# A two-block transformer forward pass on one NeuronCore: its state-space model computed in blocks of eight time steps

## The chip, the cores and the metric

The kernel runs on one core of a Trainium2 chip. The metric is device time in microseconds (us), from one launch to its end; the number quoted is the median of the timed runs.

## What is computed

A sequence of 512 tokens with 1024 features, in float32, goes through a first block (two layers, each feed-forward, mixing, feed-forward) and a second block (an even layer and an odd layer). The feed-forward is `x + 0.5 * (silu(h @ w_gate) * (h @ w_up)) @ w_down` with 2816 hidden features. The even layer joins stick-breaking attention with eight heads and a grouped state-space model (S5), which the change is about. Of the reference:

```python
def s5_mixer(u, lam_re, lam_im, log_dt, b_re, b_im, c_re, c_im, d_skip, w_glu, b_glu):
    uf = u.astype(f32).reshape(bsz, L, S5_GROUPS, S5_GROUP)      # 32 groups of 16 features
    lam = lax.complex(lam_re, lam_im)                            # 64 states to a group
    lam_bar = jnp.exp(lam * jnp.exp(log_dt)[:, None])
    b_bar = ((lam_bar - 1.0) / lam)[..., None] * lax.complex(b_re, b_im)
    bu = ...                                                     # b_bar times u, re and im
    # h[t] = lam_bar * h[t-1] + bu[t], over the 512 steps
    _, hstate = lax.associative_scan(combine, (a, bu), axis=1)
    y = c_re @ hstate.real - c_im @ hstate.imag + d_skip * uf    # per group
    y = jax.nn.gelu(y.reshape(bsz, L, S5_WIDTH))
    return y * jax.nn.sigmoid(y @ w_glu + b_glu)
```

## The kernel before

**The products.** Activations lie as features x tokens. A float32 product is made of float32r parts: every operand is split into a high and a low part, and `mm3` (L198) issues three matmuls. The high part of a weight chunk (`wh`) is made by ACT (L96, L111), the low one (`wl`) by DVE (L97, L112). `weights` (L100) loads a chunk of 256 columns by one DMA of 1 MB on SP's queue and splits it; each of `wr`, `wh` and `wl` has two buffers here, so that a chunk's split waits until PE has finished the chunk two before. `weights7`, `tokens7` and `form_a7` make the same product with seven block products where eight are usual, each of 256 columns, at the price of sums on DVE and more splits on ACT.

**The stages.** Called in order by `build` (L1606): ffn1, mix, ffn2 of layer 0; ffn1, mix, ffn2 of layer 1; the even layer; the odd layer. `ffn` (L365) works in three thirds of its hidden features (8, 8 and 6 tiles): gate and up products of a third, then its down product. A list `extra` gives other work to a feed-forward: after each of the first six down tiles of a third one function is taken, 18 in all. The tuple `ups` (from `UP7`) names the chunks whose up product is also made in seven blocks; the last feed-forward has three such chunks, the others six.

**The state-space model before.** `s5_setup` (L903) makes the scaled inputs, angles and decays in ffn1 of layer 1; its last part builds 32 steps of cosines and sines on POOL. `s5_keep` stores them in DRAM. In ffn2 of layer 1, the last feed-forward, `s5_back` reads them, and 17 steps (`s5_ahead`, L1015) make for each of 16 pairs of groups a table of cosines and sines over 512 steps (`s5_table`, ACT and DVE) and turned input weights (`s5_weights`, PE transposes). All goes to DRAM. In the even layer each pair passes through three functions of `s5_steps` (L1064): `prepare(j)` loads its tables on SP's queue, and copies its 32 features four times (L1088); `states(j)` (L1092) takes two matmuls, rotates the result on DVE and POOL, and scans 512 steps twice on DVE; `outputs` (L1117) takes eight float32 matmuls for four pairs. The core of `states`:

```python
self.tt(wr, wr, t, ALU.add, gp)          # gp: on POOL
...
for w in (wr, wi):
    nc.vector.tensor_tensor_scan(out=w, data0=r, data1=w, initial=0.0, op0=ALU.mult, op1=ALU.add)
...
self.tt(hr, hr, t, ALU.subtract, gp)
```

**The order of the work.** `even` (L1238) runs five rounds (c = 0 to 4). Four of them make q, k and v of two heads (`qk_half`, `qk_turn`, `form_b_pair`); the heads of the round before go through `logits`, `sums`, `values` and `gated`, and four pairs of the state-space model lie between them. A framework turns the program into one list for each engine, and every engine works through its own list in order. SP and ACT issue the DMAs. Eight semaphores serve all the DMAs by turns, so a DMA is issued only when the one eight before it has landed. `g` is a pool of 31 tiles of 128 x 512 used in turn: who takes a tile waits for its last reader. The head norms need `rsqrt` (L255), which is a power on POOL, in the same list as the rotations.

Of the kernel before, what the change touches and what calls it, by code (L numbers as in the profile page):

```python
# [17 lines left out]
P = 128  # L18
S = 512
# [20 lines left out]
def _bf(x):  # L40
    """Parts of 2*pi that products with whole numbers keep exact."""
    parts, rest = [], x
    for _ in range(3):
        m, e = math.frexp(rest)
        c = math.ldexp(round(m * 256), e - 8)
        parts.append(c)
        rest -= c
    return parts + [rest]


class Kern:
# [48 lines left out]
    def weights(self, src, k0=0, nk=None):  # L100
        """src: [128, k, n] of one chunk in DRAM -> its two float32r parts in SBUF."""
# [46 lines left out]
    def tokens7(self, xs, gcols):  # L148
        """The tokens' halves and their sums, to go with weights7: for each of the seven k / 2 pairs of [128, 256]."""
# [27 lines left out]
    def form_a7(self, w, x):  # L177
        """Both column tiles of a chunk, from seven products of blocks."""
# [28 lines left out]
    def form_a(self, w, j, xs, b=None):  # L207
        """features x tokens: column tile j of a chunk against the split activations."""
# [6 lines left out]
    def form_a2(self, w, xs):  # L215
        """Both column tiles of a chunk, as the activations arrive."""
# [7 lines left out]
    def form_a_late(self, w, xs, late=2):  # L224
        """Both column tiles of a chunk; the last activations as late as can be."""
# [8 lines left out]
    def form_b(self, out, w, t, xs, start=True):  # L234
        """tokens x features: token tile t against a whole chunk."""
# [24 lines left out]
    def expo(self, out, x, n):  # L260
        """exp to float32's accuracy: pow of float32's e, and the rest of e."""
# [10 lines left out]
    def setup(self):  # L272
# [7 lines left out]
        # the first chunk and the tokens by turns, as the first products take them  # L280
# [31 lines left out]
    def norm_start(self, gcols):  # L312
        """x * gain in two float32r parts; the factor of each token follows at the evacuation."""
# [10 lines left out]
    def squares(self, gcols=None):  # L324
        """Per token and partition, the sums of squares of x (times a gain)."""
# [29 lines left out]
    def rows(self, rcol, dg=None):  # L355
        """[128, 4] of token values as [128, 512], the same row in each partition."""
# [8 lines left out]
    def ffn(self, gcols, wg, wu, wd, ups, extra=(), start=False):  # L365
# [84 lines left out]
    def short_biases(self):  # L450
        """Of the two sparser dilated groups, on the keys of a block."""
# [7 lines left out]
    def toeplitz(self, row, at, step, n):  # L459
        """tile[p, c] = bias of the relative position at - step * p + c; the table runs backwards."""  # L460
# [6 lines left out]
    def lambdas(self):  # L467
# [9 lines left out]
        for l in range(DEPTH):  # L477
            # lam_init follows the difference, as in the reference; the sign serves the subtraction
# [6 lines left out]
    def dft(self):  # L485
        """The transform's tables, split."""
# [12 lines left out]
    def softmax_logits(self, b, bias, n, m):  # L499
        """logits of n keys into SBUF, their maximum into m"""  # L500
# [5 lines left out]
    def form_b_pair(self, w, t, xs, rcol, out):  # L506
        """Two token tiles of a chunk, times the tokens' factors, into out(i)."""
# [6 lines left out]
    def padded(self, b, R, view=lambda a: a, put=lambda a: a):  # L514
        """Two heads' rows apart, with zeros for the other's."""
# [1218 lines left out]
```

## Time and profile before

| | before |
|---|---|
| median of 3 runs | 3105.05 us (3104.42 to 3106.9) |
| span of the profiled execution | 3104.9 us |
| granted TensorE clock, mean | 0.993 |
| PE busy | 3044.0 us (98%) |
| DVE busy | 2151.8 us (69%) |
| ACT busy | 1398.5 us (45%) |
| POOL busy | 209.7 us (7%) |

The span runs from the first to the last instruction of one execution on the device; here it and the median differ by 0.15 us. Busy is the time in which an engine executes something; several engines are busy at once. A granted clock of 1.00 is 2.4 GHz, of 0.50 is 1.2 GHz; a value between them is a mean over a stretch.

### The profile page before, as it was taken

To read this page: it belongs to the slowest core of one execution; us is meant where nothing else is said; L and a number is where in the kernel's file an instruction comes from. 1 tells how busy PE (TensorE), PEld (TensorE's weight loads), DVE (VectorE), ACT (ScalarE), POOL (GpSimd) and SP (SyncE) were. 2 spreads that over 40 slices of the span, in tenths; PEclk is the share of its full clock that TensorE was granted. 3 is DMA by queue.
4 is the path that set the end of the run, shared out by engine and by line. 5 is a ranking of instruction groups with operands and counts; after the bars stand their busy time and mean duration, and the time that the engine had idled before them with its cause. 6 is when DMAs were issued, how large, how long until landed. Compare 5 with 4: busy or idle time off the path is not lost. (4 is left out here: it accounts for less than half of the span.)

```text
span 3104.9 us, 43951 instructions
## 1 busy us (share of the span) xinstructions
PE 3044.0 (98%) x17386; PEld 2634.1 (85%) x17386; DVE 2151.8 (69%) x3725; ACT 1398.5 (45%) x2536; POOL 209.7 (7%) x276
## 2 busy tenths in 40 slices
PE   9999999999999999999999999999999888889999
PEld 7898888888888998898989889888988877767887
DVE  7787745655577886897854656558988898765643
ACT  5343335543443344443434553345466355463532
POOL 0000000000000000010000000000000343320010
PEclk9999999999999999999999999999999999999999
DMA  4332333322223323322333322224344333212211
GB/s 152 101 109 92 106 122 113 102 94 73 104 83 108 109 89 102 112 100 105 105 123 111 110 78 102 87 77 153 118 146 144 128 104 102 77 48 80 105 69 54
DMA packets 73405, 317.95 MB, mean 102 GB/s; under 512 B 10116, under 2 KB 16260, under 8 KB 44656
## 3 DMA queue, kind: packets, MB, share of 16 engines
q1 hardware_dynamic: 55552, 286.06, 26.9%
q10 hardware_dynamic: 17648, 29.10, 3.1%
q8 instruction: 136, 2.23, 0.3%
q14 instruction: 69, 0.57, 0.1%
HBM read 292.12 MB, written 13.56 MB: 98 GB/s over the span
## 5 line engine op out<-in xcount | busy, mean ns | idle before, releaser
L200 PE MATMUL b<-xh,wh 128*128 128x512 f32 (+1 forms) x1904 | 703.8, 370 | 7.2 <-ACT xh L253 7.2
L202 PE MATMUL b<-xh,wl 128*128 128x512 f32 (+1 forms) x1904 | 694.3, 365 | 0.5 <-DVE wl L97 0.5
L201 PE MATMUL b<-xl,wh 128*128 128x512 f32 (+1 forms) x1904 | 694.0, 364 | 0.5 <-DVE xl L97 0.5
L111 ACT ACTIVATE wh<-wr 128x1024 fp32r<-128x1024 f32 (+2 forms) x402 | 389.5, 1005 | 511.8 <-PE b L201 299.4
L112 DVE TENSOR_TENSOR wl<-wr,wh 128x1024 fp32r<-128x1024 f32 (+2 forms) x402 | 464.8, 1171 | 119.4 <-ACT wh L111 117.8
L200 PE MATMUL b<-g,wh 128*128 128x512 f32 x1168 | 461.8, 395 | 0.0
L201 PE MATMUL b<-g,wh 128*128 128x512 f32 x1168 | 460.0, 394 | 0.0
L202 PE MATMUL b<-g,wl 128*128 128x512 f32 x1168 | 459.7, 394 | 0.0
L200 PEld LDWEIGHTS b<-xh,wh 128*128 128x128 f32 x1904 | 359.7, 189 | 64.6 <-ACT xh L253 7.2
L202 PEld LDWEIGHTS b<-xh,wl 128*128 128x128 f32 x1904 | 359.5, 189 | 59.6 <-DVE wl L97 0.9
L201 PEld LDWEIGHTS b<-xl,wh 128*128 128x128 f32 x1904 | 359.7, 189 | 58.3 <-issue 2.2
L243 DVE TENSOR_TENSOR g<-b,g 128x512 f32<-128x512 f32 (+2 forms) x351 | 236.5, 685 | 248.1 <-PE b L202 218.9
L202 PEld LDWEIGHTS b<-g,wl 128*128 128x128 f32 x1168 | 219.3, 188 | 51.3
L200 PEld LDWEIGHTS b<-g,wh 128*128 128x128 f32 x1168 | 219.3, 188 | 51.3 <-issue 1.2
L201 PEld LDWEIGHTS b<-g,wh 128*128 128x128 f32 x1168 | 219.4, 188 | 50.0
L201 PE MATMUL b<-wl,xh 128*128 128x256 f32 x896 | 257.5, 287 | 3.7 <-DVE wl L112 3.7
L200 PE MATMUL b<-wh,xh 128*128 128x256 f32 x896 | 259.9, 290 | 0.0
L202 PE MATMUL b<-wh,xl 128*128 128x256 f32 x896 | 256.1, 286 | 0.0
L243 DVE TENSOR_TENSOR g<-g,g 128x512 f32<-128x512 f32 (+1 forms) x287 | 208.3, 746 | 67.3 <-ACT g L253 62.5
L253 ACT ACTIVATE g<-g 128x512 f32<-128x512 f32 (+4 forms) x324 | 151.1, 479 | 116.6 <-DVE g L243 98.4
L96 ACT ACTIVATE sw<-s 128x512 fp32r<-128x512 f32 x171 | 105.8, 628 | 179.5 <-DVE s L243 153.2
L243 DVE TENSOR_TENSOR g<-g,b 128x256 f32<-128x256 f32 (+1 forms) x463 | 168.7, 398 | 22.7 <-PE b L202 20.3
(222 smaller groups left out, 5150.4 us busy)
## 6 DMA issues: line engine op xcount, KB each, us to landing
wr<-in_w_ffn_up SPq DMA_DIRECT2D x44, 1024.0 KB, 4.8
wr<-in_w_ffn_gate SPq DMA_DIRECT2D x43, 1024.0 KB, 4.8
wr<-in_w_ffn_down SPq DMA_DIRECT2D x32, 1024.0 KB, 4.9
wr<-in_w_gate SPq DMA_DIRECT2D x24, 1024.0 KB, 4.8
wr<-in_w_in SPq DMA_DIRECT2D x20, 1024.0 KB, 4.8
wr<-in_even_w_in SPq DMA_DIRECT2D x20, 1024.0 KB, 5.3
wr<-in_w_ffn_down SPq DMA_DIRECT2D x16, 768.0 KB, 4.1
g<-tb ACTq DMA_DIRECT2D x48, 256.0 KB, 3.1
```

Of the source, the lines that this page charges most:

```text
L96: self.nc.scalar.activation(hi, src, AF.Copy)
L111: nc.scalar.activation(hi[:, :, js], raw[:, :, js], AF.Copy)
L112: nc.vector.tensor_tensor(out=lo[:, :, js], in0=raw[:, :, js], in1=hi.bitcast(F32)[:, :, js], op=ALU.subtract)
L200: t.matmul(out, l[0], r[0], start=start, stop=False)
L201: t.matmul(out, l[0], r[1], start=False, stop=False)
L202: t.matmul(out, l[1], r[0], start=False, stop=stop)
L243: return (eng or self.nc.vector).tensor_tensor(out=out, in0=a, in1=b, op=op)
L253: self.nc.scalar.activation(out, a, f, **kw)
```

## The change

The state-space model is done for eight groups (a quad) at a time, in blocks of eight time steps. A block's inputs (8 steps x 16 features) lie on the 128 partitions, one column to a block. Prepared matrices carry a block's inputs to its end state, a block's start state to its outputs, and the inputs to the outputs within the block. The scan then runs over 64 blocks, and one instruction of 512 columns serves eight groups, both parts.

- `s5_setup` makes powers of lambda (0 to 8) on POOL in place of the 32 steps of the tables; it now runs in ffn2 of layer 0.
- `s5_quad(q)` (L1035) has six steps: `inputs` and `outputs` (six POOL products of 128 x 512 each), `tables` (36 small POOL products), `turn` (8 transposes), `within` (8 small matmuls), `shifted` (8 DMAs). Quads 0 and 1 lie in ffn2 of layer 0, quads 2 and 3 in ffn1 of layer 1. The last feed-forward has none, and `UP7` gives it six chunks where it had three.
- In the even layer, `feed` stores u to DRAM; `fed(c)` gathers it back by eight DMAs in runs of 64 floats; `states(c)` is 16 float32 matmuls of 64 columns, a rotation on DVE alone and one scan; `outputs(c)` is 16 float32 matmuls of 64 columns and a store; `finish(c)` gathers the result by eight DMAs.

```diff
+            self.tt(v4(re), x[0], y[0], ALU.mult, gp)       # s5_quad: product, six such, twice
...
+        def tables():
...
+            for i in range(6):
...
+                self.tt(t1, Sn[:, :, 0:n], s, ALU.mult, gp)
...
+            self.act(cc[:, 256:512], cc[:, 0:256], AF.Copy)
...
+            for i, a in enumerate((cc, ss, rr)):
+                nc.scalar.dma_start(self.s5_store[q][2 + i], a)
...
+        def shifted():
+            for e in range(8):
+                src = self.s5_pad[q][:, 16 + 16 * e:144 + 16 * e].rearrange("(g c) m -> c g m", g=8)
+                nc.scalar.dma_start(self.s5_kst[q][e * 16:(e + 1) * 16, :].rearrange("c (g m) -> c g m", g=8), src)
+        return [inputs, outputs, tables, turn, within, shifted]
...
+        def fed(q):
+            u = self.g()
+            for e in range(8):
+                src = self.s5_us[q][:, (7 - e) * 64:(8 - e) * 64].rearrange("(g c) b -> c g b", g=8)
+                nc.sync.dma_start(u[e * 16:(e + 1) * 16, :].rearrange("c (g b) -> c g b", g=8), src)
+            st[q].append(u)
+        def states(q):
...
+            for i in range(2):
+                for j in range(4):
+                    for h in range(2):
+                        g = 2 * j + h
+                        self.mm(b[h * 64:(h + 1) * 64, i * 256 + j * 64:i * 256 + (j + 1) * 64],
+                                v[i][:, j * P + h * 64:j * P + (h + 1) * 64], u[:, g * 64:(g + 1) * 64])
...
+            self.tt(w, w, t, ALU.add)
+            nc.vector.tensor_tensor_scan(out=w, data0=rr, data1=w, initial=0.0, op0=ALU.mult, op1=ALU.add)
...
             if c > 0:
                 logits(ha)
-                outputs(c - 1)
+                finish(c - 1)
             if c < 4:
-                if c > 0:
-                    states(j)
-                    prepare(j + 2)
                 self.qk_half(w, 2, xs, rcol, q)
-                if c == 0:
-                    states(j)
-                    prepare(j + 2)
+                fed(c)
                 w = self.weights(w_in[4 + c])
                 self.qk_half(w, 0, xs, rcol, k)
-                states(j + 1)
-                prepare(j + 3)
+                states(c)
...
             if c < 4:
-                states(j + 3)
+                outputs(c)
                 if c < 3:
-                    prepare(j + 5)
+                    load(c + 1)
...
-UP7 = [(3, 4, 6, 7, 9, 10)] * 3 + [(3, 4, 7)]
+UP7 = [(3, 4, 6, 7, 9, 10)] * 4
...
+        extras = [[[K.bias_loads, K.biases],
+                   [K.s5_setup, K.s5_keep, K.s5_outs, nothing, nothing, nothing] + later(0) + later(1)],
+                  [[K.s5_back, nothing, nothing, nothing, nothing, nothing] + later(2) + later(3), []]]
```

Two places in the engines' lists matter below. The first is ACT's list in ffn2 of layer 0, at the end of the second third's down product, where the next third's gate chunk is split. Before (`wh1664` is the last down chunk, `wh1675` the next gate chunk, `sw` the parts of its block sums):

```order
L111 ACTIVATE wh1664_10063<-wr1663_10061 128x8x128 [waits DMAHW1_49,PE_49,Activation_49]
L111 ACTIVATE wh1664_10063<-wr1663_10061 128x8x128
L96 ACTIVATE wh1675_10183<-wr1674_10181 128x1024 [waits DMAHW2_49,PE_49,Activation_49]
L96 ACTIVATE wh1675_10183<-wr1674_10181 128x512
L96 ACTIVATE wh1675_10183<-s1677_10189 128x512
L96 ACTIVATE sw1681_10200<-s1677_10189 128x512 [waits DVE_49]
```

The same place now (`wh1710` is the last down chunk, `wh1723` the next gate chunk; `g1699`, `g1700` and `g1701` are quad 0's tables, `s5_pad0` and `s5_kst0` tensors in DRAM):

```order
L111 ACTIVATE wh1710_10327<-wr1709_10325 128x8x128
L1133 DMA s5_cst0_8885<-g1689_10178 256x1x128 [waits Pool_49]
...
L253 ACTIVATE g1699_10230<-g1699_10230 128x256 [waits PE_49,Activation_49,Pool_49]
L253 ACTIVATE g1700_10231<-g1700_10231 128x256 [waits DMAHW6_49,DMAHW5_49,Pool_49]
...
L1106 DMA s5_rr0_8869<-g1701_10232 128x512 [waits DMAHW1_49,Pool_49]
L96 ACTIVATE wh1723_10472<-wr1722_10470 128x1024 [waits PE_49]
...
L1126 DMA s5_pad0_8893<-g1715_10370 128x256 [waits DMAHW4_49,Activation_49,Pool_49]
L1139 DMA s5_kst0_8889<-s5_pad0_8893 128x1x128 [waits DMAHW4_49]
...
L1139 DMA s5_kst0_8889<-s5_pad0_8893 128x1x128 [waits DMAHW5_49]
L96 ACTIVATE sw1729_10489<-s1725_10478 128x512 [waits DVE_49]
```

Ahead of the gate chunk's split stand now copies and stores that wait for POOL, and ahead of the split of its sums eight DMAs (the first of them waits until `s5_pad0` has landed).

The second place is SP's list in round 0 of the even layer. Before (`wr` are weights, the `g` tiles are tables and copies of u for the second pair after):

```order
L106 DMA wr3847_23445<-in_even_w_in 128x2048 [waits DMAHW3_49]
L1076 DMA g3778_23050<-s5_store_12166 128x512 [waits DMAHW4_49,PE_49]
L1076 DMA g3779_23051<-s5_store_12166 128x512 [waits DMAHW5_49,PE_49]
L1077 DMA g3780_23052<-s5_store_12166 128x256 [waits DMAHW6_49,PE_49]
L1088 DMA g3781_23056<-g3751_22871 32x512 [waits DMAHW7_49,Activation_49]
```

Now (`wr3857` is the chunk of round 1's k, `g3788` the gathered u of this round):

```order
L106 DMA wr3857_23695<-in_even_w_in 128x2048 [waits DMAHW3_49,DVE_49]
L1169 DMA g3788_23148<-s5_us0_8897 16x8x64 [waits DMAHW4_49]
L1169 DMA g3788_23148<-s5_us0_8897 16x8x64 [waits DMAHW5_49]
...
L1169 DMA g3788_23148<-s5_us0_8897 16x8x64 [waits DMAHW2_49]
L1169 DMA g3788_23148<-s5_us0_8897 16x8x64 [waits DMAHW3_49]
L106 DMA wr3878_23892<-in_even_w_in 128x2048 [waits DMAHW4_49,DVE_49]
```

The eighth gather has the semaphore of the weight load in front of the first, so it goes out when that load has landed. On PE, `states(c)` stands right behind the first half of k.

## Rows read from the trace of the kernel before

**Rows 1.** The page: busy time of each engine, share of the span, instructions.

```profile
PE 3044.0 (98%) x17386; PEld 2634.1 (85%) x17386; DVE 2151.8 (69%) x3725; ACT 1398.5 (45%) x2536; POOL 209.7 (7%) x276
```

**Rows 2.** Windows: ffn2 of layer 0, ffn1, ffn2 of layer 1, even layer; columns in line one.

```profile
core 0: us, PE busy (x) PEld busy (x) DVE busy (x) ACT busy (x) POOL busy (x), PEclk, DMA share, GB/s
853.61:1203.49 349.88, 349.88 (x2135) 312.68 (x2134) 272.42 (x454) 143.32 (x221) 1.01 (x1) 1.00 0.29 99
1203.49:1552.98 349.49, 349.49 (x2135) 312.51 (x2134) 284.51 (x512) 139.93 (x217) 12.55 (x33) 1.00 0.30 104
2045.67:2403.39 357.72, 356.73 (x2060) 312.82 (x2058) 298.31 (x563) 196.52 (x437) 6.01 (x17) 1.00 0.37 128
2403.39:2868.66 465.27, 419.31 (x2293) 343.05 (x2292) 347.49 (x496) 227.93 (x412) 140.57 (x142) 0.95 0.28 92
```

**Rows 3.** Windows: rounds 0 to 3 of the even layer; columns as in Rows 2.

```profile
2450.00:2750.00 300.00, 254.90 (x1501) 208.23 (x1501) 246.87 (x337) 139.44 (x268) 123.96 (x117) 0.93 0.28 91
```

**Rows 4.** Waits of PE in the even layer: total us, times, longest us.

```profile
PE b L269 <- DVE g L247: 16.2, 6, 4.5
...
PE b L205 <- ACT sb L253: 10.3, 3, 7.7
...
PE b L205 <- POOL g L243: 6.8, 6, 2.2
```

**Rows 5.** Groups by line, even layer: busy us, mean ns | idle before, releaser.

```profile
L243 POOL TENSOR_TENSOR g<-g,g 128x512 f32<-128x512 f32 x64 | 98.2, 1539 | 153.5 <-DVE g L243 112.4 <-PE b L205 16.0 <-PE b L202 10.0
...
L243 DVE TENSOR_TENSOR g<-g,g 128x512 f32<-128x512 f32 x72 | 65.7, 930 | 2.3 <-ACT g L253 0.7 <-PE b L205 0.6
...
L1106 DVE TENSOR_TENSOR_SCAN g<-s_r,g 128x512 f32<-128x512 f32 x32 | 49.6, 1553 | 5.7 <-POOL g L243 5.7
...
L112 DVE TENSOR_TENSOR wl<-wr,wh 128x1024 fp32r<-128x1024 f32 x38 | 49.3, 1303 | 10.9 <-ACT wh L111 10.9
...
L111 ACT ACTIVATE wh<-wr 128x1024 fp32r<-128x1024 f32 x38 | 38.2, 1047 | 40.8 <-PE b L202 30.2 <-issue 10.1 <-PE b L201 0.4
...
L205 PE MATMUL b<-g,g 128*32 128x512 f32 x64 | 13.2, 631 | 6.8 <-POOL g L243 6.8
```

**Rows 6.** Chain of waits, even layer, round 3: start us, us, what.

```profile
2685.01 1.26 POOL g L243
2686.55 1.66 POOL y L243
```

**Rows 7.** Timeline of PE: start us, us; matmuls of 512, then of 256 columns.

```profile
2425.00 0.39 PE L200 MATMUL b<-xh,wh 128*128 128x512 f32 x1
2425.22 0.39 PE L201 MATMUL b<-xl,wh 128*128 128x512 f32 x1
...
2479.97 0.28 PE L200 MATMUL b<-wh,xh 128*128 128x256 f32 x1
...
2480.09 0.28 PE L201 MATMUL b<-wl,xh 128*128 128x256 f32 x1
```

**Rows 8.** Groups by line, float32 matmuls of 64 columns in the mixing.

```profile
L205 PE MATMUL b<-g,g 128*128 128x64 f32 x96 | 11.6, 270 | 0.0
```

**Rows 9.** DMA issues, even layer: count, KB each, median us to landing.

```profile
wr<-in_even_w_in SPq DMA_DIRECT2D x17, 1024.0 KB, 5.6
```

**Rows 10.** Line 1088, copies on SP's queue: issue ns min/median/max; landing.

```profile
L1088 SPq DMA_DIRECT2D g<-g x64: 507/582/1798, 2431.9 to 2693.4; - x64
...
DMA to landing us min/median/max: 1.9/3.0/5.8
```

**Rows 11.** Groups by line, POOL's small products of the setup, in ffn1 of layer 1.

```profile
L243 POOL TENSOR_TENSOR g<-g,g 128x128 f32<-128x128 f32 x6 | 2.3, 425 | 0.0
...
L243 POOL TENSOR_TENSOR g<-g,g 128x16 f32<-128x16 f32 x5 | 1.6, 329 | 0.2
```

**Rows 12.** Line 1050, stores on ACT's queue: issue ns min/median/max; landing.

```profile
L1050 ACTq DMA_DIRECT2D s_store<-sw x16: 326/412/607, 2153.2 to 2384.0; - x16
...
DMA to landing us min/median/max: 2.0/2.3/5.6
```

**Rows 13.** Line 97, low parts of activations on DVE: ns min/median/max.

```profile
L97 DVE TENSOR_TENSOR g<-g,g x142: 420/686/1785, 39.2 to 3067.8; 128x512 fp32r<-128x512 f32 x140, 128x256 fp32r<-128x256 f32 x2
```

More of the change, by code (lines that the diff above doesn't have):

```diff
@@ new lines, in s5_setup @@
+        gp.memset(li[:, 0, :], 0.0)
+        self.tt(lr[:, 1, :], r, self.s5_c[:, 0:16], ALU.mult, gp)
+        self.tt(li[:, 1, :], r, self.s5_s[:, 0:16], ALU.mult, gp)
+        for n in (1, 2, 4):
+            a, b = slice(1, n + 1), slice(n + 1, 2 * n + 1)
+            cr, ci = (t[:, n:n + 1, :].to_broadcast([P, n, 16]) for t in (lr, li))
+            t = self.g()
+            t1, t2 = (t[:, i * 64:i * 64 + n * 16].rearrange("p (k j) -> p k j", j=16) for i in range(2))
+            self.tt(t1, li[:, a, :], ci, ALU.mult, gp)
+            self.tt(t2, li[:, a, :], cr, ALU.mult, gp)
+            self.tt(li[:, b, :], lr[:, a, :], ci, ALU.mult, gp)
+            self.tt(lr[:, b, :], lr[:, a, :], cr, ALU.mult, gp)
+            self.tt(lr[:, b, :], lr[:, b, :], t1, ALU.subtract, gp)
+            self.tt(li[:, b, :], li[:, b, :], t2, ALU.add, gp)
@@ new lines, in s5_setup @@
+        self.s5_r8 = self.const([P, 16], "s5_r8")
+        for i in range(3):
+            a = self.s5_r if i == 0 else self.s5_r8
+            self.tt(self.s5_r8, a, a, ALU.mult, gp)
+        self.s5_store = [[self.dp.tile([P, S], F32, name=f"s5_{n}{q}") for n in ("vr", "vi", "cc", "ss", "rr")]
+                         for q in range(4)]
+        self.s5_cst, self.s5_kst = ([self.dp.tile([P, 1024], F32, name=f"s5_{n}{q}") for q in range(4)]
+                                    for n in ("cst", "kst"))
@@ L1117, in outputs, with load @@
-        def outputs(j):
-            yb = self.bank()
-            for i in range(2):
-                for q in range(4):
-                    at = ((4 * j + q) % 8) * 64 + i * 32
-                    self.mm(yb[q * 32:(q + 1) * 32, :], cw[j // 2][:, at:at + 32], st[4 * j + q][i], i == 0, i == 1)
+        halves = lambda a: a.rearrange("p (i n) -> p i n", i=2)
+        blocks = lambda a: a.rearrange("p (i j b) -> p i j b", i=2, j=4)
+        def load(q):
+            st[q] = [self.g() for _ in range(9)]
+            for i in range(5):
+                nc.sync.dma_start(st[q][i], self.s5_store[q][i])
+            for i, a in enumerate((self.s5_cst[q], self.s5_kst[q])):
+                for h in range(2):
+                    nc.sync.dma_start(st[q][5 + 2 * i + h], a[:, h * S:(h + 1) * S])
@@ new lines, in outputs @@
+        def outputs(q):
+            c, k, u, s = st[q][5:7], st[q][7:9], st[q][9], st[q][10]
+            b = self.bank()
+            for g in range(8):
+                o, m = b[:, g * 64:(g + 1) * 64], slice((g % 4) * P, (g % 4 + 1) * P)
+                self.mm(o, k[g // 4][:, m], u[:, g * 64:(g + 1) * 64], True, False)
+                at = (g % 2) * 256 + (g // 2) * 64
+                self.mm(o, c[g // 4][:, m], s[:, at:at + 64], False, True)
+            y = self.g()
+            self.act(y, b, AF.Copy)
+            nc.sync.dma_start(self.s5_ys[q], y)
+            del st[q]
@@ L1133, in outputs @@
             ys.append(y)
-        return prepare, feed, states, outputs
+        return load, feed, fed, states, outputs, finish
     def sb_steps(self, heads, oa):
@@ L1245, in even @@
         us, ys, oa, heads, sz = [], [], [], {}, {}
-        prepare, feed, states, outputs = self.s5_steps(us, ys)
-        prepare(0)
-        prepare(1)
+        load, feed, fed, states, outputs, finish = self.s5_steps(us, ys)
         xs = self.norm_start(gg)
@@ L1267, in even @@
             us.append(u)
-            if i == 0:
-                feed(0)
-                feed(1)
+            feed(i)
+        load(0)
         logits, sums, values, gated = self.sb_steps(heads, oa)
@@ L1323, in even @@
                 self.form_b_pair(w, 0, xs, rcol, lambda i: v2[0][:, i * 256:(i + 1) * 256])
-                states(j + 2)
-                prepare(j + 4) if c < 3 else None
             else:
@@ L1600, with nothing @@
 NG = 31
-UP7 = [(3, 4, 6, 7, 9, 10)] * 3 + [(3, 4, 7)]
+UP7 = [(3, 4, 6, 7, 9, 10)] * 4
+def nothing():
+    pass
 def build(tc, ins, out, upto=99, first=0):
@@ L1625, in build @@
             if first:
-                for f in [K.s5_setup, K.s5_keep] + K.s5_ahead():
+                for f in [K.s5_setup, K.s5_keep, K.s5_outs] + [f for q in range(4) for f in K.s5_quad(q)]:
                     f()
```

250 lines of the change are left out of this document (133 added, 117 removed).

## The prediction

> **What bounds the kernel now.** I read the page first: PE is busy for 98% of the span, DVE for 69%, ACT for 45%, POOL for 7% [rows 1]. Means hide the stages, so I cut the span at the first matmul of each [rows 2]. The reader should see two sorts of stage. A feed-forward has PE busy to the last hundredth at a granted clock of 1.00: only less PE work makes it shorter, and any new wait of PE makes it longer. The even layer has 419.3 us of PE work in 465.3 us, at a clock of 0.95.
>
> Its four rounds hold nearly all of the loss: of 300 us PE is busy for 254.9, so it idles for 45.1, and a mean clock of 0.93 between the levels 1.2 and 2.4 GHz takes 7% of 300, 21 us, of full-speed work [rows 3]. The waits say who is late: DVE's scaling of q and k, the exponentials on ACT, POOL's rotations [rows 4]. Behind all three stand the state-space model's own instructions. POOL spends 98.2 us on its 64 sums, DVE 49.6 us on 32 scans and 65.7 us on products of two tiles at 930 ns each [rows 5]. The chain of waits shows the coupling: a rotation of 1.26 us on POOL, and only behind it, in the same list, the 1.66 us power of a head norm that the turning of q waits for [rows 6]. So rounds 0 to 3 run at the pace of DVE and POOL.
>
> **The change, part by part.** The sum is made against the profiled execution, 3104.9 us; the median, 3105.05, is the same within 0.2.
>
> *The last feed-forward* loses its 17 table steps and makes three more up products in seven blocks, as its siblings do. It takes 357.7 us, they take 349.9 and 349.5 [rows 2]: 8 us less.
>
> *The even layer, what goes.* All 64 POOL sums go, and 32 scans become 4; DVE's share per quad falls from eight scans and 32 products to one scan and about a dozen products, most of them half as wide. Of 45 + 21 = 66 us of idle time and lost clock I let 63 go; the 3 that stay are a share of the 10.3 us of waits for ACT's exponentials [rows 4], which have nothing to do with S5. This is the largest term; its lower bound is the 23 us of direct waits behind DVE and POOL in rows 4, its upper one the 66.
>
> *PE's work.* The 64 rows of 32-column outputs go, 13.2 us [rows 5], and 32 float32r matmuls of 512 columns at 0.23 us [rows 7], 7.4. In come 128 float32 matmuls of 64 columns. Each float32 matmul makes two rows (32 outputs gave 64), and 96 such rows took 11.6 us, 0.12 each [rows 8]: 31 us. Net +10; if the states' two halves of the array run side by side, +3. I take +8.
>
> *The even layer, the new wait.* `states(c)` needs all eight gathers of `fed(c)`. The eighth is issued when the 1 MB load in front of the first has landed, and that load waits for a weight buffer whose low part DVE has just taken. Count from the end of the second half of q: two high parts on ACT at 1.05 us, the last low part at 1.30 [rows 5], the load 5.6 [rows 9], the gather 3.0 [rows 10]: 12.0 us. PE has one half of k meanwhile, 48 matmuls of 256 columns at 0.12 us [rows 7], 5.8 us. So PE waits 6.2 us a round, 25 in all. Behind the gathers on SP the weight loads of the next chunks wait too; they have a whole round's work ahead of them, and I cost them at nothing. Before, the first pairs' copies had the same shape, and no wait of PE for a DMA is among rows 4; so the lower bound is 0, and the upper one adds the longest landing of rows 10 (5.8 for 3.0): 36. The store of the outputs and the gathers of `finish` have the rest of a round, and I cost them at nothing; if that cover fails, gelu is late, not PE.
>
> No row of this kernel shows a gather in runs of 256 bytes, the nearest is the 64 KB copy of rows 10. The Trainium skill, "DMA: Bandwidth & Descriptors", Specifications, puts the least size for full rate at 512 bytes and speaks of a read-modify-write below it. By that rule, were a gather to take twice its 3.0 us, the sum would be 12 us longer.
>
> Even layer: -63 + 8 + 25 = -30.
>
> *The two middle feed-forwards.* Both have no slack on PE, so what counts is what holds the splits of their weights on ACT. Quad 0 lies at the second third's down product; T is its first matmul. The transposes of `turn` come at T+22 (96 matmuls of 512 columns at 0.23). Only when they are done are the buffers free for five of POOL's products, at 1.26 [rows 6] to 1.54 us [rows 5]: 7 us. PE has 24 matmuls, 5.5 us, until `within` wants the result, which also needs a memset and four copies: about **3 us** of wait. Then 36 small POOL products at 0.33, 0.43 for the widest [rows 11], end at about T+46.5; ACT's list has their copies and three stores ahead of the next gate chunk's high part, which is ready at about T+51.7 with DVE's low part, while PE asks at T+49.5: **2.5 us**. Then a landing of 2.3 us and eight issues of 0.41 [rows 12] stand ahead of the block sums' split: **3.5 us**. That is 9 for quad 0. Quad 1, in the last third, has its tables early; its eight issues stand ahead of the next stage's first split, with nothing else for PE to do: 4.5. Quads 2 and 3 in ffn1 of layer 1 lie alike: 2 x 13.5 = 27. The turned and small matmuls add about 2. Bounds: 2, if ACT runs ahead of PE by more than I count, and 56, if each wait doubles. `s5_setup` and its powers are a third earlier and, as before, beside PE's work: ffn1 of layer 1 had them and took no longer than ffn2 of layer 0 [rows 2].
>
> Sum: -8 - 30 + 27 + 2 = **-9 us, 3096 us**.
>
> **The rivals.**
>
> *Fast (0.25).* ACT's and POOL's waits in the feed-forwards stay hidden (+8), and the gathers land in time as the copies did: even layer -47. Together -8 - 47 + 8 = -47, 3058. For it speaks that a setup with 12.55 us of POOL cost nothing [rows 2]; against it, that the old tables were on DVE and ACT, and POOL with ACT behind it is new there.
>
> *POOL and DVE hold each other up in the feed-forwards (0.19), slower.* DVE's products of two SBUF tiles take 930 ns in the even layer, beside POOL's work [rows 5]; the low parts of activations, of the same size, take 686 in the median and 1785 at most [rows 13]. If POOL's 12 products and 36 small ones of a quad, some 29 us, run at 1.8 us and 0.45, each of the three waits grows by 2 to 4 us, and DVE's low parts come later. A quad then costs 22 and 15 us, the four 74, and the sum is -8 - 30 + 74 + 2 = +38 at worst; half of that growth gives +15, 3120. It decides from 11 us a quad on average, where the forecast has 6.75: then the sum passes +6. The Trainium skill, "GPSIMD Engine Reference", Specifications, says that GpSimd shares its SBUF interfaces with VectorE, with contention where a DVE instruction has two SBUF inputs; the 930 against 686 ns agree.
>
> *The even layer gains little (0.12).* The gathers' wait at its upper bound (36) with only the 23 us of direct waits gone: -23 + 8 + 36 = +21, with the rest +42; half way there, +16, 3121. Against it: DVE and POOL lose most of their work.
>
> **How the numbers follow.** The forecast has 0.44. No change means within 6.2 us (0.2%), about what a measurement of this kernel can tell. The forecast's own spread is about -25 to +7: 0.29 of it is faster, 0.13 same, 0.02 slower. Fast adds 0.25 to faster; the two slow rivals put 0.07 in same and 0.23 in slower, with 0.01 in faster. So 0.55, 0.20, 0.25. The range of 3056 to 3122 leaves out about 1 in 10 at either end.
>
> **What would show it.** In the profile after: the last feed-forward near 350 us; POOL's work in the even layer down to its norms and selects; scans 4; the idle of PE there in four pieces of some 6 us in front of the 64-column matmuls, released by a DMA, with the clock back near 1.00; ffn2 of layer 0 and ffn1 of layer 1 at 360 to 368 us, with waits of PE for ACT's `wh` and `sw` and for the small matmuls' inputs. I am wrong if these two stay within 5 us of 349.9, if they pass 375, or if the even layer falls outside 415 to 450.

## The result, and the profile after

The changed kernel takes 3129.09 us (median of 4 runs, 3126.95 to 3134.4); the kernel before, on the same chip, 3105.57 (4 runs, 3104.42 to 3106.9). The ratio is 1.0078, with a 95% interval of 1.0064 to 1.0092: **0.8% slower, 23.5 us**. The forecast was 3096, in a range that ended at 3122.

The profiled execution has a span of 3126.9 us, 22.0 more than before. The page's line of busy times, against [rows 1]:

```profile
PE 3049.9 (98%) x17718; PEld 2653.0 (85%) x17718; DVE 2023.5 (65%) x3494; ACT 1353.8 (43%) x2357; POOL 224.9 (7%) x413
```

DVE is busy for 128 us less and PE for 6 more, so most of the 22 us is time in which PE stands still. Windows by stage say where, in the order of [rows 2] (ffn2 of layer 0, ffn1 and ffn2 of layer 1, even layer) and with their columns:

```profile
853.30:1225.84 372.54, 358.13 (x2184) 317.10 (x2182) 291.38 (x507) 146.03 (x236) 67.78 (x131) 0.99 0.32 107
1225.84:1604.91 379.07, 365.07 (x2182) 321.85 (x2183) 288.84 (x462) 152.66 (x250) 61.81 (x110) 0.97 0.32 109
2099.90:2449.48 349.58, 349.58 (x2135) 312.54 (x2134) 270.48 (x448) 138.16 (x211) 1.01 (x1) 1.00 0.29 100
2449.48:2890.92 441.44, 406.68 (x2453) 347.44 (x2452) 223.55 (x379) 225.87 (x412) 44.67 (x86) 0.96 0.28 92
```

The last feed-forward (third line) gains 8.1 us and the even layer 23.8. The two feed-forwards that now make the matrices lose 22.7 and 29.6. The mixing of layer 1 loses 2.3; the other stages move by 0.6 together.

Each stage can be split in three. Idle time is its length less PE's busy time. What the clock takes is busy time times (1 - granted clock), summed over windows of 1 us. The rest is PE's work at full clock.

| us | idle | lost to the clock | work at full clock |
|---|---|---|---|
| ffn2 of layer 0, before, after | 0.0, 14.4 | 0.0, 3.3 | 349.9, 354.8 |
| ffn1 of layer 1, before, after | 0.0, 14.0 | 0.0, 10.8 | 349.5, 354.3 |
| even layer, before, after | 45.9, 34.8 | 18.1, 9.2 | 401.2, 397.4 |

The waits of PE in the first of these (total us, times, longest us); the second stage has the same four, at 3.6, 2.6, 3.9 and 2.3 us:

```profile
PE b L205 <- ACT g L253: 3.5, 1, 3.5
PE b L202 <- DVE sw L97: 3.3, 2, 3.1
PE b L200 <- ACT wh L111: 3.2, 1, 3.2
PE b L201 <- DVE g L97: 3.0, 2, 2.3
```

In order: the small matmuls of `within` wait for copies that wait for POOL; a low part of the block sums, on DVE, is late; the next stage's first split, on ACT, is late; and DVE's low parts of activations are late. What ACT's list does about quad 0's end (start, duration, count, idle before and its releaser):

```profile
1110.33 0.84 ACT L253 ACTIVATE g<-g 128x256 f32<-128x256 f32 x2 [13.16 <-POOL g L243]
...
1117.82 5.15 ACTq L1139 DMA_DIRECT2D s_kst<-s_pad  x8
1123.02 0.63 ACT L96 ACTIVATE sw<-s 128x512 fp32r<-128x512 f32 x1 [7.01 <-DMA s_kst<-s_pad]
```

ACT waits 13.16 us for the last of POOL's small products, issues eight DMAs in 5.15 us (0.64 each, where I had 0.41 from [rows 12]), and only then makes the high part of the sums. That by itself costs PE 0.7 us. The wait of 3.1 us comes through DVE's list:

```profile
1113.03 0.69 DVE L243 TENSOR_TENSOR g<-b,g 128x512 f32<-128x512 f32 x1 [13.18 <-DMA s_cc<-g]
...
1126.73 0.69 DVE L243 TENSOR_TENSOR s<-wr 128x512 f32<-128x512 f32 x1 [2.36 <-DMA wr<-in_w_ffn_gate]
...
1128.47 0.69 DVE L97 TENSOR_TENSOR sw<-s,sw 128x512 fp32r<-128x512 f32 x1
```

DVE stands 13.18 us for a tile of `g`, until the store of quad 0's cosine table has landed. So it frees a weight buffer late, the next gate chunk is loaded from 1121.06 only, and the second low part of the sums stands behind a sum that waits for that load. The stage boundary is no plain queue either. The shifting DMAs leave ACT's list at 1219.98, but in that list the split stands also behind the high part of the last activation tile (`xh`), for which ACT waits 2.75 us, until DVE has the tile (1224.11). In the kernel before the split stands ahead of the last `xh`.

The even layer's lines by groups, against [rows 5] and [rows 8]:

```profile
L205 PE MATMUL b<-g,g 128*128 128x64 f32 x128 | 14.7, 273 | 0.0
...
L243 POOL TENSOR_TENSOR y<-y,one 128x8 f32<-128x8 f32 x8 | 13.1, 1636 | 75.6 <-DVE y L247 66.8 <-DMA g<-s_us 8.8
...
L205 PE MATMUL b<-g,g 128*64 128x64 f32 x128 | 7.9, 316 | 29.1 <-DMA g<-s_us 29.1
...
L1190 DVE TENSOR_TENSOR_SCAN g<-g,g 128x512 f32<-128x512 f32 x4 | 4.9, 1224 | 0.1
```

POOL's sums are gone and four scans are left, as announced. The scaling of q and k, POOL's rotations and the exponentials, which made [rows 4], are no longer among PE's waits; one line has taken their place:

```profile
PE b L205 <- DMA g<-s_us: 29.1, 4, 7.8
```

The chain of waits through the first of these four (start us, us, what):

```profile
2486.36 0.14 PE b L202
2486.57 1.07 ACT wh L111
2487.66 2.37 DVE wl L112 x2
2490.05 6.59 DMA wr<-in_even_w_in
2496.65 1.71 DMA g<-s_us
...
2498.66 1.97 PE b L205 x32
```

From the last matmul of the old chunk to the first of the states it is 12.3 us: a weight buffer is freed, loaded, and only behind the load does the eighth gather land. PE has 5.8 us of work meanwhile.

The clock in windows of 1 us, one after each sort of wait (columns of [rows 2]; the last but two is the granted clock):

```profile
1098.00:1099.00 1.00, 1.00 (x8) 0.66 (x3) 0.57 (x1) 0.00 (x0) 0.31 (x2) 0.50 0.79 134
1129.30:1130.30 1.00, 1.00 (x9) 1.00 (x10) 1.00 (x2) 0.00 (x0) 0.00 (x0) 1.00 0.00 0
1193.00:1194.00 1.00, 1.00 (x4) 0.81 (x3) 0.44 (x1) 0.00 (x0) 0.00 (x0) 0.50 0.00 0
1230.00:1231.00 1.00, 1.00 (x4) 0.81 (x3) 1.00 (x2) 1.00 (x3) 0.00 (x0) 0.50 0.76 319
2500.00:2501.00 1.00, 1.00 (x14) 0.88 (x12) 0.27 (x1) 0.00 (x0) 0.00 (x0) 0.50 0.00 0
```

PE is busy for the whole of each of these, but at 1.2 GHz in four of the five. They lie behind the wait of `within`, the sums' wait, that for DVE, the stage boundary and the gathers. Only the sums' wait of 3.1 us at 1126 left the clock where it was.

### The profile page after: what moved, and what is told of

Its sections match the earlier page's. It is cut to its first block, busy times and chain, and to the rows that moved or that the text cites. A ratio compares the mean times of both kernels' runs of the same rounds, so it can differ in the third digit from the quotient of the medians.

```text
span 3126.9 us, 44156 instructions
## 1 busy us (share of the span) xinstructions
PE 3049.9 (98%) x17718; PEld 2653.0 (85%) x17718; DVE 2023.5 (65%) x3494; ACT 1353.8 (43%) x2357; POOL 224.9 (7%) x413
## 4 chain that ended last, share of the span: by engine, by line
PE 88%; DVE 5%; DMA 2%; ACT 2%; POOL 1%; issue 1%; ACTq 0%; SPq 0%; DVEq 0%; POOLq 0%
PE b L202 27%; PE b L200 27%; PE b L201 27%; PE b L205 7%; PE b L269 1%; DVE g L243 1%; POOL g L243 1%; DVE wl L112 1%; ACT sb L253 1%; DMA wr<-in_even_w_in 1%; ACT g L253 1%; ACT L253 1%; DVE sw L97 0%; DMA s_cst<-g 0%; DVE wl L97 0%
## 5 line engine op out<-in xcount | busy, mean ns | idle before, releaser
L200 PE MATMUL b<-xh,wh 128*128 128x512 f32 (+1 forms) x1880 | 694.5, 369 | 14.8 <-ACT wh L111 7.2
L202 PE MATMUL b<-xh,wl 128*128 128x512 f32 (+1 forms) x1880 | 685.1, 364 | 1.5 <-DVE wl L112 1.1
L201 PE MATMUL b<-xl,wh 128*128 128x512 f32 (+1 forms) x1880 | 684.4, 364 | 1.3 <-DVE xl L97 1.3
L111 ACT ACTIVATE wh<-wr 128x1024 fp32r<-128x1024 f32 (+2 forms) x396 | 382.5, 1004 | 507.2 <-PE b L201 336.4
L243 DVE TENSOR_TENSOR g<-b,g 128x512 f32<-128x512 f32 (+2 forms) x265 | 183.7, 700 | 305.5 <-PE b L202 246.4
L243 DVE TENSOR_TENSOR g<-g,g 128x512 f32<-128x512 f32 (+3 forms) x273 | 183.2, 691 | 66.8 <-ACT g L253 62.6
L243 DVE TENSOR_TENSOR g<-g,b 128x256 f32<-128x256 f32 (+1 forms) x484 | 175.8, 397 | 19.9 <-PE b L202 17.4
```

Of the source, the lines that this page charges most:

```text
L111: nc.scalar.activation(hi[:, :, js], raw[:, :, js], AF.Copy)
L200: t.matmul(out, l[0], r[0], start=start, stop=False)
L201: t.matmul(out, l[0], r[1], start=False, stop=False)
L202: t.matmul(out, l[1], r[0], start=False, stop=stop)
L243: return (eng or self.nc.vector).tensor_tensor(out=out, in0=a, in1=b, op=op)
```

## The experiments

Three questions were put. Are the feed-forwards' losses made by the lists (what stands ahead of what: the "queues"), or by POOL and DVE slowing each other ("contention")? Is the even layer's loss the gather, and would PE go on if it came earlier? And is the half clock a price of PE's standing still? Where there is one run only, its stage windows are compared with those of the change. Stages that an edit does not touch show the scatter: ffn2 of layer 0 took 372.0 to 374.9 us in the six runs that leave it as in the change, ffn1 of layer 1 373.8 to 379.2 in five, the even layer 441.4 to 446.7 in eight (two of them load other stored tensors there).

**Half of the preparation left out.** Quads 2 and 3 are not prepared; the even layer uses 0 and 1 twice, so the order of its work stays.

```diff
-                  [[K.s5_back, nothing, nothing, nothing, nothing, nothing] + later(2) + later(3), []]]
+                  [[K.s5_back] + [nothing] * 17, []]]
```

> Quads 2 and 3 are not prepared; the even layer takes the matrices of quads 0 and 1 twice (the output is not the reference's). ffn1 of layer 1 keeps only its reading back. If the whole 29.6 us of that stage and the 2.3 us of the mixing behind it belong to the two quads, it falls to 350 and the mixing to 492.7: run about 3095. If something else made it longer (the stage's place, the pool of tiles), it stays above 360.

Measured: 3105.24 us. Windows of ffn2 of layer 0, ffn1 and mixing of layer 1:

```profile
853.21:1228.11 374.90, 360.85 (x2184) 319.03 (x2182) 291.50 (x507) 145.77 (x236) 67.73 (x131) 0.98 0.31 107
1228.11:1580.30 352.19, 351.50 (x2135) 313.75 (x2136) 277.39 (x460) 145.71 (x227) 1.02 (x1) 1.00 0.30 104
1580.30:2073.29 492.99, 492.47 (x2699) 425.33 (x2698) 275.69 (x520) 221.20 (x424) 12.35 (x13) 1.00 0.31 101
```

ffn1 falls from 379.1 to 352.2, and the mixing behind it is back at 493.0. The two quads own 27 us of that stage and the 2 us of the next one; the 2.7 us by which ffn1 still exceeds 349.5 lie at its start, behind quad 1. The run is 10 us above the 3095 expected: 5 of them lie in ffn2 of layer 0 (2.4 longer than in the change) and in the even layer (444.5 us), whose order of work it keeps.

**POOL's products alone.** `turn`, `within`, `shifted` and the quads' copies and stores on ACT are left out; the products and tables stay, nobody reads them, and the even layer loads other stored tensors in their place.

```diff
-        return [inputs, outputs, tables, turn, within, shifted]
+        return [inputs, outputs, tables, nothing, nothing, nothing]
```

> Of each quad only POOL's products and tables stay; ACT's copies, the stores, the transposes, the small matmuls and the shifting are left out, and the even layer loads other data (the output is not the reference's). Theory of the queue: PE's waits come through ACT's list and the clock behind them, so both feed-forwards fall to 350 to 356 us. Rival of contention: POOL beside DVE makes the low parts late, so at least 8 us of the 23 and 30 stay in each.

Measured: 3098.48 us; ffn2 of layer 0 takes 359.3, ffn1 of layer 1 361.1. The windows, and PE's waits in both together:

```profile
853.50:1212.77 359.27, 353.67 (x2135) 314.40 (x2134) 293.57 (x511) 143.80 (x222) 66.16 (x125) 0.99 0.29 100
1212.77:1573.85 361.08, 354.79 (x2135) 315.25 (x2134) 286.46 (x455) 140.82 (x218) 58.93 (x103) 0.99 0.29 99
```

```profile
PE b L201 <- DVE g L97: 5.3, 3, 2.3
PE b L202 <- DVE wl L112: 4.9, 2, 2.5
PE b L200 <- ACT g L96: 1.7, 2, 0.9
```

PE, ACT and DVE read none of the quads' results here, and in ffn1 DVE has 57 instructions fewer than in [rows 2]. Yet it is busy there for 2 us longer, and the stages are 9.4 and 11.6 us longer, by waits for DVE. POOL's products alone cost 21 us: 11.9 of idle time, 8.1 of lost clock, 1.0 of work. DVE's low parts in this run, and the same group in the run without POOL's products that follows (mean ns behind the comma):

```profile
L112 DVE TENSOR_TENSOR wl<-wr,wh 128x768 fp32r<-128x768 f32 x8 | 10.1, 1276 | 0.0
```

```profile
L112 DVE TENSOR_TENSOR wl<-wr,wh 128x768 fp32r<-128x768 f32 x8 | 7.6, 954 | 0.8 <-ACT wh L111 0.8
```

The down chunks' low parts lie just where the quads do: eight of them take a third longer. That is one way. The other is the pool of `g` tiles, which POOL and DVE share:

```profile
1097.99 0.69 DVE L243 TENSOR_TENSOR g<-b,g 128x512 f32<-128x512 f32 x1 [7.03 <-POOL g L243]
```

PE had ended the product that this instruction reads some 10 us before; DVE stood until POOL had let go of the tile that it writes. A low part of weights behind it came too late, and PE waited 2.5 us; the same came in ffn1. By this reading some 7 of the 21 us are waits for a tile (4.9 of idle time, 1.7 of lost clock) and some 13 lie behind slowed instructions. No run parts the two.

**The queues alone.** POOL's products and table steps are left out (the quads' values are meaningless), everything else stays in its place.

```diff
-            product(*st["x"], powers(1), [over(b) for b in self.s5_bb], ALU.subtract, ALU.add)
...
-                self.tt(t1, Sn[:, :, 0:n], s, ALU.mult, gp)
```

> The opposite: POOL's products are left out, ACT's copies, the stores, the transposes, the small matmuls and the shifting stay and read a tile that is there (the output is not the reference's). If POOL's time is what ACT waits for, the waits before the small matmuls (3.5 us) and before the gate chunk go, and about 10 of the 23 and 30 us stay for the eight DMAs in ACT's list. Rival of contention: as POOL is idle, both feed-forwards are back at 350 to 354.

Measured: 3100.21 us; the stages take 356.5 and 360.8. Their windows and the one wait of size:

```profile
853.22:1209.68 356.46, 353.25 (x2183) 314.83 (x2181) 279.40 (x507) 145.78 (x236) 12.20 (x35) 1.00 0.33 112
1209.68:1570.48 360.80, 356.65 (x2183) 317.00 (x2183) 276.67 (x462) 152.48 (x250) 4.26 (x14) 0.99 0.34 115
```

```profile
PE b L200 <- ACT wh L111: 7.2, 2, 3.9
```

So the lists and PE's own added work cost 6.6 and 11.3 us, 18 in all. Neither theory is the whole: 21 + 18 = 39 of the 52 us. The other 13 (8 to 14, if the change's two stages are taken from the other runs that leave them alone) appear only when both are there. What the change has, and neither of these two runs, is DVE's wait for the store of a quad's cosine table, 26.9 us in the two stages: POOL's products end late, ACT's copies and the store stand behind them, and DVE behind the store. How much of the 13 us it makes no run shows.

**The shifting DMAs on SP's queue.**

```diff
-                nc.scalar.dma_start(self.s5_kst[q][e * 16:(e + 1) * 16, :].rearrange("c (g m) -> c g m", g=8), src)
+                nc.sync.dma_start(self.s5_kst[q][e * 16:(e + 1) * 16, :].rearrange("c (g m) -> c g m", g=8), src)
```

> Only the eight shifting DMAs of each quad move from ACT's queue to SP's. If they hold the splits in ACT's list, the waits of PE for the sums' parts (3.1 us) and for the next stage's first split (3.2 and 3.9 us) go with their half clock: each of the two feed-forwards is 6 to 10 us shorter, the mixing behind them 2, the run about 3112. Rival: SP's queue is as full, and the weight loads behind the DMAs make PE wait there; then the run stays above 3122.

Measured: 3113.29 us; 367.4 and 368.5. PE's waits for DVE's `sw` and ACT's `wh`, 13.1 us in the change, come to 0.5; those for ACT's `sw` grow from 0.5 to 1.7. What stays is 7.1 us for `within` and 7.9 for DVE's parts. The edit moves more than the DMAs: ACT's list is another, with the next stage's first split ahead of the last `xh` (it starts at 1214.42). DVE still stands 26.2 us for the tables' stores, and no wait for `sw` comes of it, since its list has the second low part of the sums ahead of the sum that waits for the load.

**The products on DVE.** `gp` is dropped from the quads' products and tables; DVE is then busy for 9.9 and 8.8 us longer in the two stages than in the change.

```diff
-            self.tt(v4(re), x[0], y[0], ALU.mult, gp)
+            self.tt(v4(re), x[0], y[0], ALU.mult)
```

> The 48 products of each quad are made by DVE in place of POOL, at about 0.7 us for 512 columns; everything else stays. Both theories see a gain: nothing contends, and ACT's copies are ready earlier. With contention at about 10 us in each feed-forward (POOL's part alone had 9.4 and 11.6) and 6.7 for ACT's waits on POOL, the two would be at 356 and 361 us, the run about 3092. If DVE's own list is the bound instead, its 14 us a quad make the low parts late, and they stay above 365.

Measured: 3104.92 us; 360.1 and 364.5. On DVE the same 24 products take 0.69 us each and the small ones 0.16 to 0.28, and nothing else slows down:

```profile
L243 DVE TENSOR_TENSOR g<-g,g 128x512 f32<-128x512 f32 x55 | 35.5, 685 | 0.2 <-PE b L269 0.2
```

In the changed kernel POOL took 1657 ns for one of them:

```profile
L243 POOL TENSOR_TENSOR g<-g,g 128x512 f32<-128x512 f32 x24 | 39.3, 1657 | 163.0 <-DVE g L97 149.3 <-PE b L201 4.1 <-PE b L269 3.2
```

The waits left over are the two for `wh`, 12.3 us together; they go in the next run, with the eight DMAs. The run is 13 us above the 3092 expected: 4.1 and 3.5 in the two stages, 3.2 in the even layer, which the edit leaves alone.

**Both of these.**

```diff
-            self.tt(v4(re), x[0], y[0], ALU.mult, gp)
+            self.tt(v4(re), x[0], y[0], ALU.mult)
...
-                nc.scalar.dma_start(self.s5_kst[q][e * 16:(e + 1) * 16, :].rearrange("c (g m) -> c g m", g=8), src)
+                nc.sync.dma_start(self.s5_kst[q][e * 16:(e + 1) * 16, :].rearrange("c (g m) -> c g m", g=8), src)
```

> Both edits of the preparation at once: products on DVE, shifting on SP's queue. If contention, ACT's waits on POOL and the eight DMAs are all of the 52 us but PE's own 7, the two feed-forwards come to 353 to 356 us and the run to about 3080. If the gains overlap, they stay near 360.

Measured: 3094.34 us; 354.2 and 357.5. In the first stage PE idles for 0.6 us and the clock never falls. What it has above 349.9 is the turned and small matmuls, which before had no row of their own:

```profile
L269 PE MATMUL b<-cc,g 128*128 128x128 f32 x16 | 2.1, 272 | 0.0
L205 PE MATMUL b<-g,g 128*32 128x128 f32 x32 | 1.7, 278 | 0.6 <-ACT g L253 0.6
```

3.8 us a stage, 7.6 in the two, where I had written "about 2" for all four quads. The 40 us that the two stages gave back, taken from 3129, leave 3089. The other 5 are the even layer: unchanged here, it took 446.5 us instead of 441.4. With the same instructions it lost 12.9 us to the clock where the changed kernel lost 9.2, and idled 1.8 us longer.

**The gather a round earlier.** `fed(c + 1)` is issued right behind the loads of the next quad's matrices.

```diff
-                fed(c)
...
+                    fed(c + 1)
```

> The eight gathers of u go out a round earlier, right behind the loads of the quad's matrices, with no 1 MB load in front of them. If the four waits of 6.4 to 7.8 us before the states are the load's landing, as the semaphore's turn says, all 29.1 us go and the half clock behind each goes too (some 2 us each): the even layer falls from 441 to about 403 us, the run to about 3091. Rival: the gathers themselves are slow (runs of 256 bytes); then they still land late or the weight loads behind them do, and the even layer stays above 425.

Measured: 3127.95 us (3125.59 to 3131.2), ratio to before 1.0068, 1.0052 to 1.0085; the even layer 441.2, as it was. The gather is in time from the second round on, and PE waits elsewhere:

```profile
PE b L269 <- DVE g L247: 21.9, 3, 9.4
PE b L205 <- DMA g<-s_us: 4.5, 1, 4.5
```

This is the turning of q, whose head norm starts with copies on ACT. Where they stand in ACT's list:

```profile
2628.76 1.06 ACT L111 ACTIVATE wh<-wr 128x1024 fp32r<-128x1024 f32 x1 [12.21 <-PE b L202]
...
2630.24 1.04 ACT L111 ACTIVATE wh<-wr 128x1024 fp32r<-128x1024 f32 x1
2631.30 1.28 ACT L253 ACT_TABLE_LOAD   x1
2633.17 0.63 ACT L253 ACTIVATE g<-g 128x512 f32<-128x512 f32 x1 [0.59 <-DVE g L243]
2633.71 0.82 ACT L253 ACTIVATE g<-b,rce 128x256 f32<-128x256 f32 x2
```

Behind two weight splits, and behind `finish` of the round before (its table load, its gelu). The gather's wait had covered them. So the next wait was as long as the one taken away.

**Gather and finish moved.** The experiment above, and `finish(c - 1)` put behind the turning of k.

```diff
             if c > 0:
                 logits(ha)
-                finish(c - 1)
+            if c == 4:
+                finish(3)
...
+            if 0 < c < 4:
+                finish(c - 1)
```

> Early gather as before; besides, the finish of a quad (gathers, gelu) comes behind the turning of k. With the early gather alone 21.9 us of waits came up before the turning of q, whose norm stands behind a finish's gelu and two splits in ACT's list. If the gelu is what holds it, these waits fall under 8 us and the even layer to about 415; if it is the split that waits for PE, the even layer stays at about 440.

Measured: 3107.24 us; the even layer takes 424.7, 17 us less than in the change, about 10 above what was expected. The largest waits are now 6.6 us for exponentials, 4.5 for the first round's gather and 3.5 for POOL's selects. The two moves are worth something together, and the first alone nothing.

**A wait filled with matmuls.** 28 matmuls of 512 columns, read by nobody, ahead of each round's states.

```diff
+                idle = self.bank()
+                for i in range(28):
+                    self.mm(idle, xs[0][0][:, 0:P], xs[0][0])
```

> The changed kernel with 28 matmuls of 512 columns (6.4 us), whose result nobody reads, put in front of each quad's states: PE has work while it waits for the gathers, and the wait itself stays. If the half clock behind each wait is a price of PE's idling, the granted clock stays at 1.00 there and the even layer is 7 to 9 us shorter (4 x 2 us), at about 433, though PE does 26 us more work. Rival: the clock falls for another reason, or PE's waits cost only their own length; then the even layer stays at 441 or is longer.

Measured: 3124.56 us, the span 3122.8. The 25 us around the first gather, first in the change, then here:

```profile
2490.00:2515.00 25.00, 18.57 (x163) 18.28 (x162) 13.06 (x35) 8.83 (x38) 3.38 (x4) 0.86 0.24 85
```

```profile
2490.00:2515.00 25.00, 24.27 (x201) 22.78 (x200) 14.28 (x36) 10.06 (x44) 3.39 (x4) 1.00 0.32 112
...
2451.09:2886.80 435.71, 426.28 (x2565) 363.67 (x2564) 223.61 (x379) 225.50 (x411) 44.79 (x86) 0.99 0.28 93
```

The even layer takes 435.7 us, 5.7 less. The added matmuls are 26 us of work at full clock, and PE's idle time in the layer falls by as much, from 34.8 to 9.4 us. What is saved is the clock: it stays at 2.4 GHz here, and the loss to it in the layer falls from 9.2 to 2.9 us. The layer's length alone would not show it, since it scatters by 5 us; the clock at the four places does. In the eight runs that leave these waits as the change has them, 6.4 to 8.1 us long, PE started its states at 0.50 behind all 32; here, behind waits of 0.7 to 1.5 us, at 1.00 behind all four. So behind the gathers the half clock is what PE pays for standing still, and comes on top of the wait.

**The last feed-forward with three chunks in seven blocks, as before.**

```diff
-UP7 = [(3, 4, 6, 7, 9, 10)] * 4
+UP7 = [(3, 4, 6, 7, 9, 10)] * 3 + [(3, 4, 7)]
```

> The changed kernel with three up chunks in seven blocks in the last feed-forward, as before. Three chunks of 84 matmuls of 256 columns at 0.119 us become 48 of 512 at 0.23 again: the stage takes about 353 us in place of 349.6, so that of its 8.1 us some 3.4 come from the seven blocks and 4.7 from the moved tables. If the seven blocks are worth nothing without free engines, it stays at 350.

Measured: 3132.07 us; the stage takes 352.5 us. Of its 8.1 us gain 2.9 are the three up products, and 5.2 the tables that went.

**The best of all.** Products on DVE, shifting DMAs on SP's queue, gather and finish moved: the diffs of the two pairs above together, of which the first lines are

```diff
-            self.tt(v4(re), x[0], y[0], ALU.mult, gp)
+            self.tt(v4(re), x[0], y[0], ALU.mult)
...
-                fed(c)
```

> All four edits: products on DVE, shifting on SP's queue, early gather, late finish. If the stages are independent, the two feed-forwards take 354 and 358 us, the mixing 495, the even layer 425: 3072 to 3076, faster than both kernels. If the even layer's gain needs waits elsewhere, it stays above 3085.

Measured: 3077.48 us (4 runs, 3075.76 to 3079.37) against 3105.97; ratio 0.9907, 0.989 to 0.9923. **It is 28.5 us faster than the kernel before**, and 1.5 above the range expected. The two feed-forwards take 354.2 and 357.5 us; the even layer took 430.7 where 425 was expected:

```profile
2410.62:2841.27 430.65, 408.07 (x2453) 346.73 (x2452) 221.38 (x379) 233.44 (x419) 50.99 (x86) 0.98 0.28 94
```

With the same layer in the run of the two moves alone it was 424.7. Of the 6 us, 5.7 are lost clock (9.0 here, 3.3 there); idle time is the same within 0.8.

## Why the prediction was wrong

| term | forecast | measured |
|---|---|---|
| last feed-forward | -8 | -8.1 |
| even layer: idle time and lost clock that go | -63 | -49.1 |
| even layer: the gathers' wait | +25 | +29.1 |
| even layer: PE's work | +8 | -3.8 |
| two feed-forwards: PE's waits | +27 | +28.4 |
| two feed-forwards: lost clock | 0 | +14.1 |
| two feed-forwards: PE's added work | +2 | +9.7 |
| mixing of layer 1, rest | 0 | +1.7 |
| sum | -9 | +22 |

**The step that failed** is in "The two middle feed-forwards": "That is 9 for quad 0 ... 2 x 13.5 = 27", put into the sum as 27 us. Waits came, and as long in sum as that (28.4). But they were charged by their length alone. Behind each of the large ones but one PE worked for 3 to 7 us at 1.2 GHz, and lost 14.1 us by it in all. That this belongs to the standing still the filled wait shows for the gathers; for the shorter waits of the feed-forwards it is inferred, not shown. The row that would have priced it was on the table: in [rows 3] 45.1 us of idle time went with 21 us of lost clock (18.1 by 1-us windows, since the 21 counted idle time too). The text let that clock come back where waits left, and charged none where waits came. The 27 + 25 us of new waits at the same rate are 21 to 24 us more, hence 3117 to 3120. The two stages and the even layer measured 14.1 + 9.2 = 23.3.

A second term was mis-sized in the same stages: "The turned and small matmuls add about 2" came without a row, and measured 9.7, of which 7.6 are those matmuls by their own rows.

The same step is why the even layer gave 24 and not 30: "with the clock back near 1.00" was wrong (0.96), 9.2 us stayed lost behind the gathers, and 5.7 us of other idle time stayed where I had 3. Against that, the states' two halves do run side by side: 128 rows in 7.9 us, 0.06 each, beside 0.115 for those of the outputs. I had named that case (+3) and taken the dearer one. And those 7.9 us were run at 0.50, right behind the wait: with the wait filled the same 128 rows took 4.6 us. Some of the old outputs' 13.2 us was at half clock too. Counted at full clock, each matmul up to the next one's start, the states are 3.8 us and the outputs 14.0; before, the outputs were 10.6 and the 32 matmuls of 512 columns 8.3: a net of -1.1. The rest of the -3.8 is spread over matmuls that both kernels have (1.3 of it in the turning of q and k), and no row tells its cause.

**The gathers' wait** came out by its own steps. The chain of the first has 12.3 us where the text counted 12.0; PE's cover was 5.8 as counted. The pieces differ: 3.4 us for the splits as written, 6.6 for the load (5.6), and 1.7 for the last gather (3.0). In the other rounds it was 7.4 to 7.8, and the chain is led there by the exponentials. The Trainium skill, "DMA: Bandwidth & Descriptors", Specifications, puts the least transfer for full rate at 512 bytes; the trace does not bear it out as a cost on this path, since the last gather, in runs of 256 bytes, landed 1.7 to 2.0 us after the load, under the 3.0 of [rows 10]. The median of all 32 gathers, from issue to landing, was 4.6 us, but seven of each eight go out beside the 1 MB load.

**The feed-forwards' waits, one by one.** That their sum met the 27 is in good part luck. `within`: 3 expected, 3.5 and 3.6 measured, by the path that the text gives. The sums: 3.5 expected, 3.3 and 2.6, but most of it through DVE's list and a late load. The stage boundary: 4.5 expected, 3.2 and 3.9, but behind the last `xh` and not behind the eight issues alone. The gate chunk behind the tables' copies: 2.5 expected, not there; its split was early enough, at 1112.34. In its place stand waits for DVE's low parts, 3.0 and 2.3 us, which the text had only in a rival. And that a quad's tables keep DVE waiting for a tile of `g` is in no part of the text.

**The rivals.** *POOL and DVE hold each other up* (0.19, 3120 us) came nearest by its mechanism, which is shown in part: POOL's products alone cost 21 us, some of it by tiles that POOL held. It was to decide from 11 us a quad, and the quads cost 52.2 / 4 = 13. But it had the growth in the waits' length, and what came beyond the waits forecast was 14.1 us of lost clock and 9.7 of PE's work. The Trainium skill, "GPSIMD Engine Reference", Specifications, has GpSimd and VectorE share their SBUF interfaces; the trace agrees: eight low parts took 954 ns each without POOL's products and 1276 beside them. *Fast* fell at its first condition, *the even layer gains little* did not come (441 is inside "415 to 450"). Of the signs named, "if they pass 375" was met by ffn1 of layer 1, at 379.

## What to carry to other kernels

Price a new wait of a busy PE as its length plus the half clock behind it, from a row of the same kernel that has both. In a stage without slack, moved side work costs by what stands ahead of the next split in each engine's list, by whose instructions it slows, and by whose tiles it holds; leave out each part alone, since here the two parts together cost a fifth to a third more than their sum. A wait that is taken away shows the one it covered: the gather moved alone gave nothing, and with the next list entry moved too 17 us.

## What the runs showed of the hardware

- After some waits of 2.3 to 4 us PE ran at 0.50 for 3 to 7 us, and lost up to as much again as the wait had taken (3.1 us behind the 3.2 at 1225). In ffn1 of layer 1 a wait of 2.4 us at 1503 was followed by 0.50, in ffn2 of layer 0 one of 3.1 us at 1126 by 1.00. What tells them apart no run here settles.
- The same even layer, instruction by instruction, took 441.4 us in the change and 446.5 in the run with products on DVE and shifting DMAs on SP; 3.7 us of that is lost clock. With gather and finish moved it took 424.7 and 430.7 in two runs; 5.7 us of that is lost clock.
- Issuing one shifting DMA of 16 partitions held ACT's list for 0.64 us, where a plain store of 128 x 512 took 0.41 [rows 12].
- A product of two 128 x 512 tiles costs DVE 0.69 us; on POOL it took 1.66 in the mean, and two of them 5.89 us at the worst (from 1165.01 on), beside DVE's work.
- Behind waits for the gathers of 6.4 to 8.1 us PE ran at 0.50 in 32 of 32 cases, behind waits of 0.7 to 1.5 us in the same places at 1.00 in four of four.
